# Lo halves of the down weights: a negated copy on ScalarE and an adding DMA in place of VectorE's subtraction

## The chip, the cores and the metric

The kernel runs on one core of one Trainium2 chip. The core has a matrix engine (TensorE, PE in the profile; its weight loads are PEld), VectorE (DVE), ScalarE (ACT), GpSimd (POOL), and SyncE (SP), which issues most of the DMAs. Each engine runs its own instructions in their order and waits on semaphores for the others. 16 DMA engines move data between DRAM and the on-chip memory (SBUF). The metric is the device time of one execution in microseconds, as the median of several runs.

## The reference

A decoder trunk of two layers on 256 tokens of width 1024. Each layer is a SwiGLU FFN, a mixer (causal pooling beside a gated linear recurrence), and a second SwiGLU FFN, each followed by a layer norm. What matters here is the FFN, of which there are four:

```python
D_MODEL = 1024; SEQ = 256; DEPTH = 2
D_FF = ((8 * D_MODEL // 3 + 127) // 128) * 128          # 2816

def swiglu(x, w_gate, w_up, w_down):
    return (jax.nn.silu(x @ w_gate) * (x @ w_up)) @ w_down

# per layer l
x = layer_norm(ALPHA * x + 0.5 * swiglu(x, ffn1_gate[l], ffn1_up[l], ffn1_down[l]), ln_g[l, 0], ln_b[l, 0])
...                                                     # mixer, layer norm
x = layer_norm(ALPHA * x + 0.5 * swiglu(x, ffn2_gate[l], ffn2_up[l], ffn2_down[l]), ln_g[l, 2], ln_b[l, 2])
```

All inputs and the output are float32.

## The kernel before

A float32 operand is split into two float32r halves: hi, the rounded value, and lo, what the rounding left (the value minus hi). A product of two such operands is three matmuls, hi·hi, hi·lo and lo·hi (`mm3`, L95 to L99; the one at L97 reads the lo half of the weight). Everything that PE multiplies, weights above all, is first split in this way by `halves` (L101): ACT writes hi as a rounding copy (L102), DVE writes lo as source minus hi (L103).

Weights come as tiles of 128 x 1024 float32, 512 KB each. Every weight of the program is one `Weight` object, and all of them stand in one list, `stream`, in the order of their use. `advance` (L144) loads from this list as long as the next one finds room, never past one that does not. `Weight.load` (L116) takes a buffer `raw` (five of them, shared by all weights), two buffers for hi and lo from the ring of its kind, issues the load on SP's queue (L128) and splits it (L129). There are three rings: "w" with 8 pairs of buffers (gate and up weights, and the mixer's weights), "x" with 2 more pairs for gate and up weights, and "d" with 6 pairs for the down weights, whose halves are named `dh` and `dl`. A pair comes free when PE has used the weight for both halves of the tokens (`used`, L137).

An FFN (class `FFN`, L289) has 11 groups of 256 hidden columns. Each group needs four gate and up tiles and two down tiles, so there are 22 down tiles in an FFN and 88 in the program. A group's hidden values are made by `GT` (L311, tokens as columns, matmuls at L330) or by `G` (L306, matmuls through `mm3`), pass through `gate_turned` or `gate`, where ACT and DVE compute the silu and the product and split it into `hth` and `htl`, and are multiplied with the down weights in `D` (L452), once for each half of the tokens, into the accumulators `acc`. `D(g, 0)` is the first use of group g's down weights. The first FFN begins with `start` (L375), where pieces of the weights and of x arrive together. In all other FFNs the down weights of groups 0 and 1 are loaded right behind group 1's gate weights; the d ring lies in a scope that is opened anew behind each mixer (`open_ffn`, L149), while the two FFNs that follow one another without a mixer between them share it.

PE's order is written out by hand (`manual_schedule`, L88), with a queue of delayed steps (`Later`, L45) that places transposes and the mixer's small products between the large matmuls. The order on the other engines is planned when the program is built, from priorities and estimated times; loads have a lower priority (`BEHIND`, L145), the gate's instructions a higher one (`AHEAD`, L350). A few splits are pinned to the program's order: the ACT copy for the first ten weights of the stream, and the DVE subtraction of the next few weights after each layer norm (`pinned`, L130 to L134).

GpSimd has little to do: it issues three small DMAs in `lower_bounds` (L563, L565), copies and clears some tiles in the mixer, and computes the power -1/2 in each layer norm (L250) and head norm (L794). The layer norm's last two DVE instructions (L254) wait for that power.

## Time and profile before

| | |
|---|---|
| median of 3 runs | 950.89 us (950.67 to 950.92) |
| span of the profiled execution | 948.8 us |
| what lies around the span, against the median | 2.1 us |
| mean granted clock of TensorE | 0.998 |
| busy: PE, PEld, DVE, ACT, POOL | 99%, 85%, 69%, 54%, 2% of the span |
| DMA | 180.05 MB, mean 190 GB/s; SP's queue 55.6% of 16 engines |

The profile gives no time of the profiled execution beside its span; the difference to the median is taken as what lies around it. "Busy" of an engine is the time in which one of its instructions runs; PE's matmuls overlap, and a matmul of 512 columns takes about 390 ns from start to end while the next starts some 227 ns later. In the rows of a group, the number after the bar is the total busy time in us and the mean duration of one instruction in ns, then the time that its engine was idle before it, and who ended that idleness. In the rows of a timeline the first number is the start in us from the beginning of the span and the second the duration of the row (of all its instructions, where it says x2 or more). In the rows of DMA issues the last number is the median time from issue to landing in us.

### The profile page before, as it was taken

The numbers are of one execution on the slowest core, as the hardware profiler recorded it, in microseconds if no ns is written. First come the engines' busy times: TensorE is split into PE (matmuls) and PEld (weight loads), VectorE is DVE, ScalarE is ACT, GpSimd is POOL, SyncE is SP. The second block draws the span as 40 slices with busy tenths as digits, with TensorE's granted clock in tenths as the row PEclk, the third lists the DMA queues.
The fourth block names the chain that finished last, engine by engine and source line by source line (L and its number), as shares of the span: only waits on it lengthen the run. The fifth ranks groups of instructions, "written<-read, shape, count | busy, mean of one in ns | idle before, by whom it ended". The sixth has DMA issues, their size and how long they took to land.

```text
span 948.8 us, 13285 instructions
## 1 busy us (share of the span) xinstructions
PE 939.1 (99%) x4911; PEld 803.2 (85%) x4911; DVE 653.3 (69%) x1089; ACT 514.7 (54%) x816; POOL 23.7 (2%) x38
## 2 busy tenths in 40 slices
PE   9999999999999999999999999999999999999996
PEld 7888888888988888888888888888898888888885
DVE  7885666669879765655776565647899797565625
ACT  7675554368546755454445645533975466646420
POOL 0000000000010000000000000000000000000000
PEclk9999999999999999999999999999999999999999
DMA  8877676333627876655446666443417387676301
GB/s 309 308 270 261 245 241 195 107 104 118 228 85 257 299 240 208 207 186 178 137 157 237 222 224 208 168 156 101 145 56 264 117 270 253 228 230 211 114 1 45
DMA packets 50944, 180.05 MB, mean 190 GB/s; under 512 B 6208, under 2 KB 6464, under 8 KB 50880
## 3 DMA queue, kind: packets, MB, share of 16 engines
q1 hardware_dynamic: 50544, 178.55, 55.6%
q8 instruction: 38, 0.62, 0.3%
q0 software_dynamic: 192, 0.53, 0.2%
q14 instruction: 26, 0.21, 0.1%
q10 hardware_dynamic: 144, 0.13, 0.0%
HBM read 178.14 MB, written 1.05 MB: 189 GB/s over the span
## 4 chain that ended last, share of the span: by engine, by line
PE 97%; DVE 1%; DMA 1%; ACT 0%; issue 0%; DVEq 0%; ACTq 0%
PE gu L330 39%; PE acc L98 10%; PE acc L97 10%; PE acc L96 10%; PE gu L96 7%; PE gu L97 7%; PE gu L98 7%; PE gu L824 1%; PE acc L405 1%; PE gu L178 1%; PE acc L750 1%; PE acc L696 1%; DMA raw<-in_wout 1%; PE gu L445 0%; PE gu L429 0%; PE acc L786 0%
## 5 line engine op out<-in xcount | busy, mean ns | idle before, releaser
L102 ACT CAST wh<-raw 128x1024 fp32r<-128x1024 f32 x196 | 205.3, 1053 | 114.0 <-DMA raw<-in_gu 45.0
L103 DVE TENSOR_TENSOR wl<-raw,wh 128x1024 fp32r<-128x1024 f32 x196 | 236.1, 1220 | 20.6 <-ACT wh L102 11.7
L330 PE MATMUL gu<-xt,wh 128*128 128x512 f32 x800 | 188.1, 390 | 0.0
L330 PEld LDWEIGHTS gu<-xt,wh 128*128 128x128 f32 x800 | 150.1, 188 | 32.2
L103 DVE TENSOR_TENSOR dl<-raw,dh 128x1024 fp32r<-128x1024 f32 x88 | 106.8, 1223 | 99.2 <-ACT dh L102 98.3
L102 ACT CAST dh<-raw 128x1024 fp32r<-128x1024 f32 x88 | 91.9, 1049 | 113.1 <-DMA raw<-in_dn 109.3
L96 PE MATMUL acc<-dh,hth 128*128 128x512 f32 x354 | 138.8, 392 | 0.0
L98 PE MATMUL acc<-dh,htl 128*128 128x512 f32 x354 | 138.0, 390 | 0.0
L97 PE MATMUL acc<-dl,hth 128*128 128x512 f32 x354 | 137.6, 389 | 0.0
L96 PE MATMUL gu<-wh,xt 128*128 128x512 f32 x288 | 114.2, 396 | 0.0
L97 PE MATMUL gu<-wl,xt 128*128 128x512 f32 x288 | 112.6, 391 | 0.0
L98 PE MATMUL gu<-wh,xt 128*128 128x512 f32 x288 | 112.5, 391 | 0.0
L330 PE MATMUL gu<-xt,wl 128*128 128x256 f32 x800 | 103.5, 282 | 0.0
L330 PEld LDWEIGHTS gu<-xt,wl 128*128 128x128 f32 x800 | 100.6, 191 | 2.1
L353 DVE TENSOR_TENSOR sil<-gu,sil 128x256 f32<-128x256 f32 x66 | 27.8, 421 | 88.4 <-ACT sil L352 88.4
L98 PEld LDWEIGHTS acc<-dh,htl 128*128 128x128 f32 x354 | 66.5, 188 | 13.9
L97 PEld LDWEIGHTS acc<-dl,hth 128*128 128x128 f32 x354 | 66.6, 188 | 12.4
L96 PEld LDWEIGHTS acc<-dh,hth 128*128 128x128 f32 x354 | 66.6, 188 | 12.2
L98 PEld LDWEIGHTS gu<-wh,xt 128*128 128x128 f32 x288 | 54.1, 188 | 11.8 <-DVE xt L103 0.2
L97 PEld LDWEIGHTS gu<-wl,xt 128*128 128x128 f32 x288 | 54.2, 188 | 10.6
L96 PEld LDWEIGHTS gu<-wh,xt 128*128 128x128 f32 x288 | 54.1, 188 | 10.7
L330 PE MATMUL gu<-xt,xh 128*128 128x512 f32 x256 | 62.7, 395 | 0.0
(187 smaller groups left out, 1071.5 us busy)
## 6 DMA issues: line engine op xcount, KB each, us to landing
raw<-in_gu SPq DMA_DIRECT2D x172, 512.0 KB, 4.4
raw<-in_dn SPq DMA_DIRECT2D x88, 512.0 KB, 4.5
raw<-in_win SPq DMA_DIRECT2D x40, 512.0 KB, 4.3
raw<-in_wout SPq DMA_DIRECT2D x16, 512.0 KB, 4.6
lng<-in_ln_g SPq DMA_DIRECT2D x6, 512.0 KB, 4.9
lnb<-in_ln_b SPq DMA_DIRECT2D x6, 512.0 KB, 6.2
x<-in_first SPq DMA_DIRECT2D x4, 384.0 KB, 3.7
raw<-in_first SPq DMA_DIRECT2D x4, 384.0 KB, 4.7
```

The costliest lines, as they stand in the source:

```text
L96: nc.tensor.matmul(ps, lh, wh, start=start, stop=False)
L97: nc.tensor.matmul(ps, lh, wl, start=False, stop=False)
L98: nc.tensor.matmul(ps, ll, wh, start=False, stop=stop)
L102: first = nc.scalar.copy(dst_h, src)
L103: return first, nc.vector.tensor_tensor(dst_l, src, dst_h.bitcast(F32), ALU.subtract)
L178: nc.tensor.transpose(pt[:, k - a, :], self.nat[:, k * P:(k + 1) * P], ident)
L330: nc.tensor.matmul(ps[i][part][:, 2 * S - w:], weight.parts[lo][:, c:c + P], x[:, 0:w], start=kt == 0 and not lo, stop=kt == KT - 1 and lo ...
L353: nc.vector.tensor_tensor(dst, p[:, 0:S], dst, ALU.add)
L405: nc.tensor.matmul(ps[i][part][:, 2 * S - w:], ws[k // 2].parts[lo][:, c:c + P], xs[:, 0:w], start=k == 0 and not lo, stop=k == KT - 1 and ...
L696: nc.tensor.matmul(pe[:, a:], lf[hf][c][:, h * P:(h + 1) * P], cumM[:, c, a:], start=True, stop=True)
L750: nc.tensor.matmul(dst[:, 2 * j:2 * j + 2, :], side[:, j, :], E[:, 2 * j:2 * j + 2, t0:t0 + dst.shape[2]], start=True, stop=True)
L824: nc.tensor.matmul(ps[i // 2][:, i % 2, :], w, x, start=kt == 0 and n == 0 and i % 2 == 0, stop=kt == KT - 1 and n == 2 and i % 2 == 1)
```

## The change

Only the loads of the down weights (ring "d") change. The load of `raw` on SP's queue stays, and ACT's rounding copy into `dh` stays. Then ACT runs a second instruction that reads `dh` and writes it with its sign turned into `dl`, and GpSimd issues a DMA that reads the weight a second time from DRAM and adds it onto `dl` in SBUF. DVE's subtraction is no longer made for these tiles. The gate, up and mixer weights, and the splits of activations, go through `halves` as before. The pinning to the program's order is kept for the ACT copies of the first weights; for the second instruction of a split it now holds only where that is DVE's subtraction.

```diff
             if not self.by_hand:
                 nc.sync.dma_start(raw, self.src)
-                first, second = halves(wh, wl, raw)
-                if position[0] < STARTED + 6:
+                if self.ring == "d":
+                    first = nc.scalar.copy(wh, raw)
+                    if position[0] < STARTED + 6:
+                        tc.keep_in_program_order(first)
+                    nc.scalar.activation(wl, wh.bitcast(F32), AF.Copy, scale=-1.0)
+                    second = nc.gpsimd.dma_start(wl, self.src, accum_op=ALU.add)
+                else:
+                    first, second = halves(wh, wl, raw)
+                if position[0] < STARTED + 6 and isinstance(second.ins, mybir.InstTensorTensor):
                     tc.keep_in_program_order(first)
-                if pinned[0]:
+                if pinned[0] and isinstance(second.ins, mybir.InstTensorTensor):
                     tc.keep_in_program_order(second)
                 pinned[0] = max(0, pinned[0] - 1)
```

## The prediction

> **What bounds the kernel now.** I read the engine totals first, then the chain that ended last, then the waits of TensorE (PE), and only then the places where the changed instructions meet PE. The engine totals and the chain's first line:

> ```profile
> span 948.8 us, 13285 instructions
> PE 939.1 (99%) x4911; PEld 803.2 (85%) x4911; DVE 653.3 (69%) x1089; ACT 514.7 (54%) x816; POOL 23.7 (2%) x38
> ...
> PE 97%; DVE 1%; DMA 1%; ACT 0%; issue 0%; DVEq 0%; ACTq 0%
> ```

> PE is busy for 939.1 of 948.8 us and carries 97% of the chain. The waits view for PE alone has two rows in the whole execution:

> ```profile
> PE gu L429 <- DVE zero L426: 1.1, 1, 1.1
> PE acc L769 <- DVE Pm L762: 0.8, 1, 0.8
> ```

> So PE waited 1.9 us for anybody: 1.1 at the very start, 0.8 in the second mixer. Neither has to do with down weights. Any change that only frees another engine can give back at most those 1.9 us, 0.2% of the time, and a change that makes PE wait anywhere adds that wait in full, because nothing later runs faster to make it up. The question is therefore not how much VectorE (DVE) saves but whether a `dl` now arrives after PE wants it.

> The time is made against the profiled execution: span 948.8, median of the runs 950.89, so 2.1 us lie around the span; I keep them unchanged.

> **What is removed.** The groups by line of the two instructions that make a down weight:

> ```profile
> L103 DVE TENSOR_TENSOR dl<-raw,dh 128x1024 fp32r<-128x1024 f32 x88 | 106.8, 1223 | 99.2 <-ACT dh L102 98.3
> L102 ACT CAST dh<-raw 128x1024 fp32r<-128x1024 f32 x88 | 91.9, 1049 | 113.1 <-DMA raw<-in_dn 109.3
> L354 ACT ACTIVATE sil<-sil 128x256 f32<-128x256 f32 x68 | 28.4, 421 | 5.4 <-DVE sil L353 5.3
> L102 ACT CAST hth<-hn 128x256 fp32r<-128x256 f32 x68 | 27.7, 409 | 18.8 <-DVE hn L355 17.2
> ```

> 88 subtractions of 1223 ns leave DVE: 106.8 us, 653.3 to about 546. PE is never held by them, so their removal is worth 0 on the path. A `raw` buffer of a down weight also comes free at the end of ACT's cast and not of DVE's subtraction, so the SyncE (SP) load queued behind it can start one to three microseconds sooner; PE waits for no load now, so this too is worth 0.

> **What is added.** (a) 88 activations on ScalarE (ACT), 128x1024 each. No row shows that form; the cast of the same size takes 1049 ns, and at 128x256 an ACTIVATE takes 421 against a cast's 409, so I take 1.05, between 1.0 (back to back, where starts overlap) and 1.1. That is 92 us, ACT 515 to 607 of 949. ACT works 9.67 us in the 17 us of a late group (the 416 to 433 stretch below), so two more per group fit there. (b) 88 DMAs on GpSimd (POOL), each behind its activation. (c) 88 times 512 KB more from DRAM, beside the load of `raw`, which stays. The price of (b) is the unknown. The nearest rows, POOL's own DMAs, an SP load of the same 256 KB, the down-weight loads in the first 34 us, and the queue totals:

> ```profile
> 190.66 0.58 POOL L565 DMA_DIRECT2D la<-rows  x1 [2.88 <-DMA rows<-both]
> la<-rows POOLq DMA_DIRECT2D x1, 256.0 KB, 3.6
> pw<-in_pw SPq DMA_DIRECT2D x2, 256.0 KB, 3.9
> raw<-in_dn SPq DMA_DIRECT2D x4, 512.0 KB, 5.0
> q1 hardware_dynamic: 50544, 178.55, 55.6%
> ```

> Call L the time from POOL's issue to the landing of one `dl`. Lower end: 3.6, what a POOL DMA of half the bytes without an add took. Upper end: 10.0, two whole loads of 5.0 one after the other, as if destination and source were fetched in turn. Between them: 55.6% of 948.8 is 527.5 us of all 16 engines for 178.55 MB, so 512 KB (0.524 MB) are 1.55 us of engine time. An addition has to read what it adds to, so I count the crowded load of 5.0 and one more pass of 1.55: L = 6.5. That is nearer the lower end because the two reads should stream together, as the loads do now.

> The two 256 KB rows give POOL's queue no handicap against SP's (3.6 against 3.9). [...]

> **Where it meets PE.** I matched each of the 88 `dl`, in the order of the code, with its first matmul. Three first pairs of the four FFNs come close. The first FFN's (timelines of ACT, DVE, PE):

> ```profile
> 20.54 2.03 ACT L102 CAST dh<-raw 128x1024 fp32r<-128x1024 f32 x2
> 22.74 3.49 DVE L103 TENSOR_TENSOR dl<-raw,dh 128x1024 fp32r<-128x1024 f32 x3
> 27.83 0.40 PE L97 MATMUL acc<-dl,hth 128*128 128x512 f32 x1
> 28.52 0.39 PE L97 MATMUL acc<-dl,hth 128*128 128x512 f32 x1
> ```

> The second `dl` is done near 25.1 now, 3.4 us ahead of 28.52. After the change ACT does two casts and two negations from 20.54, in whichever order: 20.54 + 4 x 1.0 = 24.5. So 4.0 us are left for L: a wait of 6.5 - 4.0 = 2.5 us.

> The FFN behind the first mixer, its first pair, with POOL's row of the layer norm:

> ```profile
> 290.57 1.05 ACT L102 CAST dh<-raw 128x1024 fp32r<-128x1024 f32 x1 [0.44 <-DMA raw<-in_dn]
> 292.26 1.00 POOL L250 TENSOR_TENSOR rs<-rs,neghalf 128x1 f32<-128x1 f32 x1 [13.32 <-DVE rs L249]
> 293.42 1.41 DVE L254 SCALAR_TENSOR_TENSOR x<-x,rs,lnb 128x512 f32<-128x512 f32 x2
> 296.90 1.04 PE L178 MATMUL gu<-ident,x 128*128 128x128 f32 x8
> 292.80 0.39 ACT L363 ACTIVATE sil<-gu 128x256 f32<-128x256 f32 x1
> 298.36 1.22 DVE L103 TENSOR_TENSOR dl<-raw,dh 128x1024 fp32r<-128x1024 f32 x1
> 300.08 0.39 PE L97 MATMUL acc<-dl,hth 128*128 128x512 f32 x1
> ```

> Here DVE finishes the second `dl` at 299.58, only 0.5 us ahead. After the change: 290.57 + 4 x 1.0 + 0.4 for the silu between = 295.0; 5.1 us are left for L, a wait of 1.4 us. The FFN behind the second mixer repeats it:

> ```profile
> 760.10 1.05 ACT L102 CAST dh<-raw 128x1024 fp32r<-128x1024 f32 x1 [0.16 <-DMA raw<-in_dn]
> 769.42 0.39 PE L97 MATMUL acc<-dl,hth 128*128 128x512 f32 x1
> ```

> 760.10 + 4.4 = 764.5, 4.9 left, a wait of 1.6 us. At both places POOL computes a layer norm's power (292.26 to 293.26) just as the first DMA becomes ready (292.6), so that DMA waits 0.65 us; the second pair member sets the wait and is free of it. If the planner puts the DMA first, the power comes about 1.3 us late, and the transposes that need it start at 296.90, 2.1 us after the normalised rows are done now (293.42 + 1.41 = 294.83), so it is covered.

> All other pairs are covered: the next closest are the second pair of the same two FFNs (ready 303.4, used 313.60) and the first pair of the third FFN:

> ```profile
> 301.02 2.36 DVE L103 TENSOR_TENSOR dl<-raw,dh 128x1024 fp32r<-128x1024 f32 x2
> 313.60 0.39 PE L97 MATMUL acc<-dl,hth 128*128 128x512 f32 x1
> 467.42 2.35 DVE L103 TENSOR_TENSOR dl<-raw,dh 128x1024 fp32r<-128x1024 f32 x2
> 484.73 0.39 PE L97 MATMUL acc<-dl,hth 128*128 128x512 f32 x1
> ```

> 10 and 15 us of cover stand against L plus one activation less one subtraction, about 6.4. The loads behind must not starve either. Bandwidth by stretch (columns: stretch, length, busy of PE, PEld, DVE, ACT, POOL, clock, DMA share, GB/s):

> ```profile
> 20.00:40.00 20.00, 20.00 (x105) 17.10 (x104) 18.35 (x23) 14.50 (x23) 0.00 (x0) 1.00 0.82 279
> 416.00:433.00 17.00, 17.00 (x92) 14.69 (x91) 9.93 (x15) 9.67 (x16) 0.00 (x0) 1.00 0.59 199
> ```

> A late group leaves 41% of 17 us, 7.0 us of DMA, for two additions of 1.55 to 3.1 each: it fits. At 20 to 40 us only 3.6 us are free for four additions, so gate weights there land a few microseconds later; PE, itself 2.5 us late, gives them as much back, so I add nothing.

> **Sum.** 2.5 + 1.4 + 1.6 = 5.5 us: span 954.3, time 950.89 + 5.5 = 956.4. With L = 3.6 all three waits vanish, 950.9. With L = 10.0 they are 6.0 + 4.9 + 5.1 = 16.0, 966.9.

> **Rivals.** First, no slower: the added DMA lands as fast as a plain load (L up to 5.0), the second pair member arrives on time behind both mixers, and only the first FFN waits, up to 1.0 us: 950.9 to 951.9. For it: the POOL row of 3.6 and DMA engines that have gaps; against it: that row has half the bytes and no add. It ends where L passes 5.2 (1.2 + 0.1 + 0.3 = 1.6).

> Second, much slower: the adding runs well below the copy rate. An add costing 3.5 us of all engines or more exceeds the 7.0 us free in a late group, `dl` falls behind group by group, and waits like L = 12 (8.0 + 6.9 + 7.1 = 22) give 973 or more. For it: nothing shows the rate of an add; against it: a late `dl` has 10 us of cover and more, so only the three starts and the crowded first FFN would show it.

> [...]

> Fourth, faster: less DVE work removes the 0.8 us wait before L769 and the planner's new order costs nothing: 950.1 at best, since PE cannot do its 939.1 us of work sooner.

> **Chances and range.** The forecast (L 5.2 to 10) 0.55; no slower 0.20; much slower with or without the clock 0.21; faster 0.04, of which hardly any passes the bound. A measurement of this kernel can tell about 0.2%, 1.9 us, from no change. So faster 0.03, same 0.21, slower 0.76. The range runs from just under L = 3.6 to the upper end of L with a first clock loss: 950.7 to 969.

> **What would show it.** Right: PE's waits gain three rows for `dl`, all before the first pair in the FFNs at about 28, 300 and 769 us; DVE near 546, ACT near 607; POOL's issue to landing 5.2 to 10 us; no new PE wait in late groups. Wrong: issue to landing under 5 (then nothing is lost), DMA share near 1.00 in late groups, clock below 1.00 behind a wait, or PE waits for `gu` weights or behind a layer norm, which I priced at nothing.

## The result and the profile after

The changed kernel takes 1023.64 us (median of 4 runs, 1018.12 to 1025.66) against 950.83 us before: a ratio of 1.0755, 95% interval 1.0731 to 1.0780. It is slower, as forecast, but by 72.8 us where 5.5 were forecast, and far above the upper end of the range (969). The profiled execution took 1025.38 us with a span of 1023.6, 74.8 more than the span before.

Engine totals and the DMA queue that grew, from the page after:

```profile
span 1023.6 us, 13365 instructions
...
PE 968.2 (95%) x4911; PEld 816.7 (80%) x4911; DVE 552.0 (54%) x1001; ACT 588.8 (58%) x904; POOL 99.7 (10%) x126
...
q0 software_dynamic: 12864, 46.67, 24.7%
```

PE does the same 4911 matmuls, but is busy for 29.1 us more (968.2 against 939.1) and idle for 45.7 us more (55.4 against 9.7). These two add up to the 74.8. So there are two questions: whom did PE wait for, and why did the same matmuls take longer? Queue q0, GpSimd's, carried 0.53 MB and took 0.2% before. Now 24.7% of 1023.6 us over the 88 adds is 2.87 us of all 16 engines for one add (the few DMAs that were there before make 0.02 us of it).

The two largest rows of PE's waits (before, the view had the two that the prediction shows):

```profile
PE gu L337 <- DVE sil L360: 25.2, 13, 4.6
PE acc L97 <- DMA dl<-in_dn: 20.0, 6, 5.2
...
```

The second row is the one that the prediction has: six waits for `dl`, two in each of the three first pairs, but 20.0 us where 5.5 were forecast. The first row it hasn't: 13 times PE stands before the gate and up matmuls (L337, L330 before the change) because DVE has not yet read the tile `gu` (L360) that they overwrite, in PSUM, the memory that PE writes its results to.

The longer matmuls are a matter of the granted clock. Three stretches behind the three first pairs, PE alone (stretch, length, busy of PE with its count, clock, DMA share, GB/s):

```profile
33.17:43.41 10.24, 7.10 (x16) 0.50 1.05 276
336.95:343.78 6.83, 4.78 (x11) 0.50 1.06 276
831.89:842.13 10.24, 6.70 (x15) 0.50 1.06 276
```

The clock is 0.50 there, and half of the 18.6 us of work, 9.3 us, is lost. Eight more such stretches, 3.41 us each, stand behind gate waits. PE works for 45.2 us in all eleven, so the clock explains 22.6 of the 29.1 us; the other 6.5 are not explained here.

Where the loss accrues is seen when each PE matmul of a `dl` is set against the same one before. Its lateness (us, worked out from the starts of the 354 matmuls L97 in both traces) grows from 0 to 12.1 in the first pairs of the first FFN, to 32.1 at that FFN's end, by 9.1 in the first pairs of the second, 10.4 in the rest of it, 9.3 in the third FFN, 9.2 in the first pairs of the fourth and 5.1 behind them: 75.2 in all. First pairs cost 30.4 of this, the rest 44.8.

How a gate comes late shows in the timelines of ACT and PE in the first FFN:

```profile
93.32 1.05 ACT L130 CAST dh<-raw 128x1024 fp32r<-128x1024 f32 x1 [5.91 <-DMA raw<-in_dn]
94.28 1.04 ACT L102 CAST wh<-raw 128x1024 fp32r<-128x1024 f32 x1
95.22 1.05 ACT L133 ACTIVATE dl<-dh 128x1024 fp32r<-128x1024 f32 x1
...
100.03 0.36 ACT L359 COPY sil<-gu 128x256 f32<-128x256 f32 x1
```

```profile
100.91 1.46 PE L337 MATMUL gu<-xt,wh 128*128 128x512 f32 x3 [3.70 <-DVE sil L360]
```

ACT stands 5.91 us before the cast of a down weight whose load is late. The cast and six more instructions for weights stand in ACT's order ahead of the gate's first copy at 100.03, DVE's part (L360) comes behind that, and PE, which ran out of free `gu` tiles at 97.2, waits 3.70 us. The load that ACT waits for is one of two issued at 84.3 and 84.7 us:

```profile
raw<-in_dn SPq DMA_DIRECT2D x2, 512.0 KB, 10.1
```

Before, the median of these loads was 4.5 us. The DMA engines are full here: their share is 1.00 from 82 to 88 us and 1.05 from 88 to 94 (a packet counts whole in the stretch in which it starts, so a share can pass 1). By stretch of the same work, before and then after (columns as in the prediction's table; the first FFN from its start-up on, and the second, third and fourth FFN):

```profile
20.00:172.00 152.00, 152.00 (x806) 131.05 (x805) 101.80 (x145) 88.07 (x141) 0.00 (x0) 1.00 0.72 245
...
299.00:484.00 185.00, 185.00 (x948) 157.60 (x947) 122.16 (x172) 97.44 (x148) 1.84 (x2) 1.00 0.62 210
484.00:655.00 171.00, 171.00 (x882) 145.91 (x881) 102.50 (x146) 88.24 (x136) 0.92 (x1) 1.00 0.56 188
...
768.00:945.00 177.00, 173.08 (x891) 147.61 (x890) 105.95 (x158) 80.50 (x129) 1.84 (x2) 1.00 0.50 168
```

```profile
20.00:204.00 184.00, 163.13 (x810) 136.66 (x809) 78.07 (x125) 108.88 (x164) 19.52 (x22) 0.94 0.91 268
...
332.00:535.00 203.00, 191.34 (x944) 160.61 (x944) 93.53 (x146) 115.93 (x173) 21.57 (x25) 0.97 0.86 247
535.00:715.00 180.00, 175.09 (x876) 147.38 (x875) 81.45 (x128) 102.80 (x155) 16.64 (x19) 0.98 0.83 240
...
829.00:1020.00 191.00, 178.65 (x887) 150.16 (x887) 81.41 (x136) 95.76 (x149) 18.38 (x21) 0.96 0.75 212
```

Before, the first FFN kept the DMA engines busy for 0.72 x 152 = 109 us. Its 22 adds of 2.87 are 63 more: 172 us of work for 152 us of time. As long as these transfers stay in this stage, some of them land late, whatever order the engines work in.

### The profile page after: what moved, and what is told of

Read it like the earlier page. It is cut to its first block, busy times and chain, and to the rows that moved or that the text cites. A ratio compares the mean times of both kernels' runs of the same rounds, so it can differ in the third digit from the quotient of the medians.

```text
span 1023.6 us, 13365 instructions
## 1 busy us (share of the span) xinstructions
PE 968.2 (95%) x4911; PEld 816.7 (80%) x4911; DVE 552.0 (54%) x1001; ACT 588.8 (58%) x904; POOL 99.7 (10%) x126
## 3 DMA queue, kind: packets, MB, share of 16 engines
q1 hardware_dynamic: 50544, 178.55, 49.7%
q0 software_dynamic: 12864, 46.67, 24.7%
HBM read 224.27 MB, written 1.05 MB: 220 GB/s over the span
## 5 line engine op out<-in xcount | busy, mean ns | idle before, releaser
L102 ACT CAST wh<-raw 128x1024 fp32r<-128x1024 f32 x196 | 205.0, 1048 | 106.6 <-PE gu L98 48.0
L103 DVE TENSOR_TENSOR wl<-raw,wh 128x1024 fp32r<-128x1024 f32 x196 | 236.3, 1221 | 40.1 <-ACT wh L102 30.1
L337 PE MATMUL gu<-xt,wh 128*128 128x512 f32 x800 | 205.0, 412 | 24.5 <-DVE sil L360 23.5
L337 PEld LDWEIGHTS gu<-xt,wh 128*128 128x128 f32 x800 | 158.0, 199 | 66.4 <-DVE sil L360 28.0
L360 DVE TENSOR_TENSOR sil<-gu,sil 128x256 f32<-128x256 f32 x66 | 27.8, 421 | 259.2 <-ACT sil L359 259.2
L97 PE MATMUL acc<-dl,hth 128*128 128x512 f32 x354 | 141.6, 400 | 20.0 <-DMA dl<-in_dn 20.0
L96 PE MATMUL acc<-dh,hth 128*128 128x512 f32 x354 | 141.3, 399 | 0.0
L98 PE MATMUL acc<-dh,htl 128*128 128x512 f32 x354 | 141.0, 398 | 0.0
L134 POOL DMA_DIRECT2D dl<-in_dn x88 | 77.2, 877 | 634.0 <-ACT dl L133 367.7
L97 PE MATMUL gu<-wl,xt 128*128 128x512 f32 x288 | 113.1, 393 | 0.0
L337 PE MATMUL gu<-xt,wl 128*128 128x256 f32 x800 | 103.5, 283 | 0.0
L337 PEld LDWEIGHTS gu<-xt,wl 128*128 128x128 f32 x800 | 100.6, 191 | 2.0
L97 PEld LDWEIGHTS acc<-dl,hth 128*128 128x128 f32 x354 | 68.2, 193 | 35.5 <-DMA dl<-in_dn 22.9
L133 ACT ACTIVATE dl<-dh 128x1024 fp32r<-128x1024 f32 x88 | 92.5, 1056 | 0.7
L337 PE MATMUL gu<-xt,xh 128*128 128x512 f32 x256 | 63.8, 398 | 1.8 <-DVE sil L360 1.8
L98 PEld LDWEIGHTS gu<-wh,xt 128*128 128x128 f32 x288 | 54.4, 189 | 11.8 <-DVE xt L103 0.2
## 6 DMA issues: line engine op xcount, KB each, us to landing
raw<-in_gu SPq DMA_DIRECT2D x172, 512.0 KB, 5.7
raw<-in_dn SPq DMA_DIRECT2D x88, 512.0 KB, 5.1
dl<-in_dn POOLq DMA_DIRECT2D x88, 512.0 KB, 8.6
raw<-in_win SPq DMA_DIRECT2D x40, 512.0 KB, 5.0
raw<-in_wout SPq DMA_DIRECT2D x16, 512.0 KB, 4.6
lng<-in_ln_g SPq DMA_DIRECT2D x6, 512.0 KB, 6.0
lnb<-in_ln_b SPq DMA_DIRECT2D x6, 512.0 KB, 8.2
```

What stands on the lines that cost most here:

```text
L96: nc.tensor.matmul(ps, lh, wh, start=start, stop=False)
L97: nc.tensor.matmul(ps, lh, wl, start=False, stop=False)
L98: nc.tensor.matmul(ps, ll, wh, start=False, stop=stop)
L102: first = nc.scalar.copy(dst_h, src)
L103: return first, nc.vector.tensor_tensor(dst_l, src, dst_h.bitcast(F32), ALU.subtract)
L133: nc.scalar.activation(wl, wh.bitcast(F32), AF.Copy, scale=-1.0)
```

## The experiments

Two theories and a rival stood at the start. L: the first adds of an FFN land too late (the `dl` row). T: the traffic of the adds makes later loads late, and through ACT's order the gate. O: the 88 extra ACT instructions and the planner's new order make the gate late without any traffic. Each experiment is told with its change to the changed kernel, unless it says otherwise. All were timed beside the kernel before on the same chip.

**No DMA, the negation kept.**

```diff
-                    second = nc.gpsimd.dma_start(wl, self.src, accum_op=ALU.add)
+                    second = nc.vector.tensor_tensor(wl, raw, wl.bitcast(F32), ALU.add)
```

> The changed kernel, but VectorE adds the loaded weight onto the negated tile; no added DMA. ACT keeps its second instruction for each down weight, and the planner orders ACT and DVE anew. Theory T (traffic: the adding DMAs make later loads of raw late, ACT stands in order before a cast that waits for its load, the gate behind it is late, TensorE waits for a free PSUM bank) and theory L (the first adds of an FFN land too late): neither has anything left here, so 951 to 955. Rival O (ACT's 88 extra instructions and the new order on ACT and DVE make the gate late by themselves): the waits of PE for the gate stay, 26 us of them and some 13 us of half clock behind them, so 980 to 992.

The two conditions on pinning ask for `self.ring != "d"` in this kernel, so that the same instructions are pinned as in the changed kernel. 952.28 us, ratio 1.0016 (1.0006 to 1.0025). The page and the waits:

```profile
PE 940.1 (99%) x4911; PEld 802.6 (84%) x4911; DVE 653.0 (69%) x1089; ACT 589.2 (62%) x904; POOL 23.7 (2%) x38
```

```profile
PE gu L337 <- DVE sil L360: 0.2, 1, 0.2
```

ACT has the work that it has in the changed kernel (589.2 against 588.8), and the gate waits are 0.2 us. The extra ACT instructions cost 1.5 us at most. The planner's order is another one here, since DVE has its 88 instructions back, so the half of O that blames the order is left to the copy below.

**An eighth of each add.**

```diff
-                    second = nc.gpsimd.dma_start(wl, self.src, accum_op=ALU.add)
+                    second = nc.gpsimd.dma_start(wl[:, 0:128], self.src[:, 0:128], accum_op=ALU.add)
```

> The changed kernel, but each adding DMA covers columns 0 to 127 of 1024, so that the output leaves out seven eighths of the addition: the same instructions on the same engines, an eighth of the bytes. T: the DMA share falls back near that of before and the waits for the gate go; L: an add lands in 3 to 5 us, the waits for dl go; both together 951 to 957. O: the waits for the gate stay, 980 to 992. If the dl waits come from the way GpSimd issues (a fixed cost per DMA) and not from bytes, issue to landing stays above 8 us and about 34 us of the loss stay: 985.

960.46 us, ratio 1.0097 (1.0082 to 1.0112): above the 957 of T and L, far below the 980 of O. The waits for the gate are gone, those for `dl` not wholly; O's 88 ACT instructions are all still there (waits of PE, then DMA issues):

```profile
PE acc L97 <- DMA dl<-in_dn: 5.0, 6, 2.5
```

```profile
raw<-in_gu SPq DMA_DIRECT2D x172, 512.0 KB, 4.7
raw<-in_dn SPq DMA_DIRECT2D x88, 512.0 KB, 4.3
dl<-in_dn POOLq DMA_DIRECT2D x88, 64.0 KB, 4.2
```

A DMA of 64 KB still takes 4.2 us, nearly as long as the loads of 512 KB. So the latency behind the first waits is only partly one of its own bytes.

**A copy instead of an add.**

```diff
-                    second = nc.gpsimd.dma_start(wl, self.src, accum_op=ALU.add)
+                    second = nc.gpsimd.dma_start(wl, self.src)
```

> The changed kernel, but the DMA copies the weight over the negated tile instead of adding, so that the subtraction is left out: the same reads from DRAM, the same order, no read of the destination. If the price is the addition itself (2.87 us of all 16 engines against 1.5 for a copy): DMA share near 0.80 in late groups, issue to landing 5 to 6 us, most waits go: 952 to 965. If the price is the second read from DRAM, of whatever kind: little changes, 1005 to 1025. In between: the waits at the three starts go by half (L about 6 to 8) and the gate waits stay, 985.

975.30 us, ratio 1.0255 (1.0236 to 1.0275), between the low case and the middle one. Of the middle case the first half came (the waits for `dl` fall from 20.0 to 11.8 us), the second did not (the gate waits nearly go) (the page's queue and DMA issue, then the waits of PE):

```profile
q0 software_dynamic: 12864, 46.67, 14.8%
...
dl<-in_dn POOLq DMA_DIRECT2D x88, 512.0 KB, 6.5
```

```profile
PE acc L97 <- DMA dl<-in_dn: 11.8, 6, 3.3
PE gu L337 <- DVE sil L360: 3.1, 2, 2.5
```

14.8% of 972.3 us over 88 is 1.64 us of engine time for a copy, against 2.87 for an add of the same bytes. That the DMA adds, and does not only copy, is worth 1023.6 - 975.3 = 48.3 of the 72.8 us. ACT, DVE and GpSimd run the same instructions in the same order in this kernel as in the changed one (904, 1001 and 126, compared place by place in the two traces). So neither the order nor ACT's negations, both of which are still there, can account for the 48.3 us, and O falls.

The landing of the second member ends the waits of a first pair. Its issue to landing in the first, second and fourth FFN, first with the add, then the copy, then the eighth of an add (each one DMA):

```profile
dl<-in_dn POOLq DMA_DIRECT2D x1, 512.0 KB, 10.7
...
dl<-in_dn POOLq DMA_DIRECT2D x1, 512.0 KB, 11.1
...
dl<-in_dn POOLq DMA_DIRECT2D x1, 512.0 KB, 12.4
```

```profile
dl<-in_dn POOLq DMA_DIRECT2D x1, 512.0 KB, 7.7
...
dl<-in_dn POOLq DMA_DIRECT2D x1, 512.0 KB, 8.3
...
dl<-in_dn POOLq DMA_DIRECT2D x1, 512.0 KB, 9.3
```

```profile
dl<-in_dn POOLq DMA_DIRECT2D x1, 64.0 KB, 5.9
...
dl<-in_dn POOLq DMA_DIRECT2D x1, 64.0 KB, 6.0
...
dl<-in_dn POOLq DMA_DIRECT2D x1, 64.0 KB, 6.3
```

Means of 11.4, 8.4 and 6.1: of 11.4 us some 6 are there with an eighth of the bytes, 2.3 more come with the rest of the bytes and 3.0 with adding instead of copying. Why 64 KB take 5.9 to 6.3 us at these places was not isolated.

**The first two groups of each FFN without the add.**

```diff
-                if self.ring == "d":
+                if self.ring == "d" and not self.soon:
...
-                    self.dw[n] = [Weight(dn[2 * n + i], "d", ND) for i in range(2)]
+                    self.dw[n] = [Weight(dn[2 * n + i], "d", ND, soon=n < 2) for i in range(2)]
```

> The changed kernel, but the first four down weights of each FFN get their lo half from VectorE as before (16 of 88); the other 72 keep the adding DMA. L and T are separate losses: the 20.0 us of waits for dl and the 13.7 us of half clock behind them go, the waits for the gate stay: about 990. If the waits for dl cause the others too (everything later is displaced by them): 955 to 970. If removing them gains nothing, because the loads behind were only hidden by these waits: 1010 or more.

995.50 us, ratio 1.0465 (1.0436 to 1.0493), within 6 us of the first case:

```profile
PE gu L338 <- DVE sil L361: 28.5, 14, 5.4
```

No wait for `dl` is left, and the gate waits (one line further down in this kernel) are about as they were, 28.5 us against 25.2. L and T are separate: 28 us for the first pairs, by lateness 30.4, and 44.7 for the rest, by lateness 44.8.

**The traffic alone.** The kernel before, and beside it an add (then a copy) of each down weight onto a spare tile:

```diff
                 first, second = halves(wh, wl, raw)
+                if self.ring == "d":
...
+                    extra = nc.gpsimd.dma_start(spare, self.src, accum_op=ALU.add)
+                    tc.add_manual_dep(extra.ins, first.ins.name,
...
```

> The kernel before, whole, and besides it for each down weight an adding DMA from GpSimd's queue, issued behind ACT's rounding copy, onto a spare tile that nobody reads; one spare tile, so an add starts when the one before it has landed. ACT has no second instruction, and nothing waits for the adds. If the traffic of the adds alone makes the loads, and through ACT's order the gate, late: waits of PE for the gate of 15 to 30 us and half clock behind them, 970 to 995. If the loads become late but VectorE's old share of the work and the old order absorb it (the loss needs ACT's negation standing between cast and gate as well): 951 to 958.

> As the run with the spare add, with a plain copy in place of the add: the same bytes from DRAM, about half the engine time. If it is the time that the DMA engines spend, and not the bytes from DRAM, that makes the loads late: 951 to 955, whatever the spare add shows. If the bytes: as the spare add within 5 us.

1050.48 us (ratio 1.1059, 1.1005 to 1.1114) and 986.74 us (1.0382, 1.0329 to 1.0435): the traffic alone costs more than the change. The waits of PE with the add, then with the copy:

```profile
PE gu L341 <- DVE sil L364: 46.6, 28, 4.6
PE gu L456 <- DVE hn L375: 15.1, 3, 13.3
```

```profile
PE gu L341 <- DVE sil L364: 11.6, 10, 2.6
PE gu L456 <- DVE hn L375: 9.2, 3, 6.9
```

With ACT's and DVE's old work and nobody waiting for the adds, the gate waits come in full: the traffic alone makes the gate late, as T has it. Both numbers missed, though: the add is above the range, and the copy is not 951 to 955, so engine time alone does not decide. Part of the excess belongs to the experiment: with one spare tile each DMA waits on POOL for the one before, and a layer norm's power stands behind it. In the run with the add:

```profile
548.84 0.88 POOL L133 DMA_DIRECT2D spare<-in_dn  x1 [5.11 <-DMA spare<-in_dn]
549.40 0.90 POOL L261 TENSOR_TENSOR rs<-rs,neghalf 128x1 f32<-128x1 f32 x1
```

That is the 13.3 us in the row for `hn`. The larger gate waits (46.6 against 25.2) fit with `raw`, which here comes free only after DVE's subtraction, while the changed kernel frees it behind ACT's cast; that was not isolated.

**Half of the adds.** The kernel without adds in the first two groups, and of every other pair only the second weight keeps its add.

```diff
-                    self.dw[n] = [Weight(dn[2 * n + i], "d", ND, soon=n < 2) for i in range(2)]
+                    self.dw[n] = [Weight(dn[2 * n + i], "d", ND, soon=n < 2 or i == 0) for i in range(2)]
```

> The kernel in which the first four down weights of each FFN go through VectorE (995.5), and of the others only the second of each pair keeps the adding DMA: 36 adds, not 72. If each add costs its share (44.7 us for 72): 973. If the loss begins where the DMA engines are full (share 0.9 and more in the late groups, which 36 adds bring to about 0.75): 951 to 960.

962.75 us, ratio 1.0120 (1.0090 to 1.0151): 12.0 us for 36 adds where 72 cost 44.7. It lies 2.8 us above the full-engine case and 10 below the case of equal shares.

Four kernels can now be set against the filling of the DMA engines. For each FFN, need is the DMA time before plus its adds or copies by their engine time (2.87; 1.64 for a copy; 3.07 in the last kernel, from 11.5% of 962.0 us over 36), over the FFN's time before; the loss is the growth of the lateness without the first pairs:

| kernel | first FFN | second | third | fourth |
|---|---|---|---|---|
| changed | 1.13: 20.0 us | 0.96: 10.4 | 0.93: 9.3 | 0.86: 5.1 |
| no adds in the first two groups | 1.06: 18.6 | 0.90: 9.0 | 0.86: 11.6 | 0.79: 7.0 |
| copy | 0.96: 3.9 | 0.81: 0.0 | 0.77: 0.2 | 0.70: 0.0 |
| every other add | 0.90: 8.6 | 0.77: 0.1 | 0.72: 3.9 | 0.66: 1.2 |

Above 1 the loss is heavy. Between 0.7 and 1 the mean does not decide alone: in these four kernels adds lose where copies at the same filling do not; why was not tested by itself. The spare copies, which are not in the table, do not fit it: at the copy's filling of 0.96 they lost 12.2 us in the first FFN, 7.7 of it in waits for the gate, where the copy lost 3.9. So the filling is not all that counts; what else does was not isolated.

**The waits filled with work.** In the first, second and fourth FFN, ahead of the first pair:

```diff
+                    if g == 0 and hf == 0 and c == 0 and self.ln != (1, 0):
+                        for _ in range((14, 9)[i]):
+                            nc.tensor.matmul(self.accs[hf][1], ht[i][0], dw[i][0][:, cs], start=True, stop=True)
                     mm3(self.accs[hf][c], ht[i][0], ht[i][1], dw[i][0][:, cs], dw[i][1][:, cs],
```

> The changed kernel, with more work for PE: in the first, second and fourth FFN 14 more matmuls ahead of the first pair of down weights and 9 ahead of its second member (3.2 and 2.0 us at 0.227 us each), into an accumulator that is cleared before its use; the output stays the same. They fit into waits for dl of 5.2 and 2.2, 3.2 and 2.8, 4.4 and 2.2 us. If the granted clock is halved because PE stood idle: the spells of 10.2, 6.8 and 10.2 us at half clock behind these waits go, which is worth half of 27.3: 1010 to 1013 from 1023.6, less work per time but sooner. If the half clock comes from something else that goes on there (the DMA burst, the load on the chip): 1023 to 1026, spells as before. If the fillers only add: 1030 or more.

1025.98 us, ratio 1.0774 (1.0724 to 1.0823). The time is that of "something else", the trace is not:

```profile
PE 976.8 (95%) x4980; PEld 823.7 (80%) x4980; DVE 551.3 (54%) x1001; ACT 589.9 (57%) x904; POOL 100.3 (10%) x126
```

```profile
PE gu L337 <- DVE sil L360: 34.7, 15, 7.7
PE acc L97 <- DMA dl<-in_dn: 5.0, 5, 2.2
```

Behind the first pairs 3.4 us at half clock are left of 27.3. PE is busy for 8.6 us more with 69 more matmuls of 0.227 us (15.7 us), so 7.1 us of clock came back, of 9.3 by PE's work (the expectation took half of all 27.3 us); but the gate waits grew by 9.5 us, most of them in the first FFN (7.7 us at 76.7). With the loads setting the pace there, the earlier PE only waited for longer.

**The same, with the copy.** There the first FFN's filling is 0.96, not 1.13.

```diff
+                        for _ in range((9, 7)[i]):
+                            nc.tensor.matmul(self.accs[hf][1], ht[i][0], dw[i][0][:, cs], start=True, stop=True)
```

> The kernel with a copy in place of the add (975.3; it leaves out the subtraction), with 9 and 7 more matmuls of PE ahead of the first pair of down weights in the first, second and fourth FFN (2.0 and 1.6 us), into an accumulator that is cleared before its use. There the waits for dl were 3.3 and 1.0, 1.6 and 1.6, 2.8 and 1.6 us and half clock behind them cost about half of 13.5 us of work. Now the DMA engines have room in the first FFN, unlike in the changed kernel with filled waits. If standing idle halves the clock: spells shrink from 17.1 us to 6.8 or less, PE busy without the fillers falls by 4 to 7 us, and little of it is given back: time 970 to 974, though 48 matmuls (10.9 us) are added. If idleness is not the cause: spells as before and 976 to 980, since the fillers do not fit wholly. If every lead gained is given back at the gate: 975 to 980 with spells gone.

967.18 us, ratio 1.0184 (1.0161 to 1.0206), against 975.30 with 48 matmuls fewer: more work, and 8 us sooner, below even the range.

```profile
PE 951.3 (99%) x4959; PEld 811.4 (84%) x4959; DVE 551.3 (57%) x1001; ACT 589.4 (61%) x904; POOL 70.6 (7%) x126
```

Without the 10.9 us of fillers PE is busy for 940.4 us, 7.8 less than in the copy kernel and 1.3 more than before, and no stretch at half clock is left before the end: the mean granted clock is 0.998, as before the change, against 0.99 in the copy kernel. With PE's idleness filled, the half clock went.

**A longer descriptor space.** In the changed kernel the fourth add of an FFN is issued only when the first lands (in the first FFN ready at 31.8 us, issued at 34.3, the first landed at 34.1).

```diff
-    nc = bacc.Bacc("TRN2", target_bir_lowering=False, num_devices=1, dynamic_dma_scratch_size=1024)
+    nc = bacc.Bacc("TRN2", target_bir_lowering=False, num_devices=1, dynamic_dma_scratch_size=4096)
```

> The changed kernel with four times the space for the descriptors of GpSimd's DMAs (4096 in place of 1024), so that a fourth add need not wait for the landing of the first. If the DMA engines' time sets the loss: 1019 to 1030, with the fourth add of an FFN issued earlier but landing no earlier. If GpSimd's queue held adds back: 990 to 1010.

1025.48 us, ratio 1.0795 (1.0751 to 1.0840), no change:

```profile
PE gu L337 <- DVE sil L360: 24.3, 13, 4.6
PE acc L97 <- DMA dl<-in_dn: 17.8, 6, 4.8
```

The fourth add is now issued at once (31.6) and takes 13.0 us instead of 11.2; in both kernels it lands 11.4 to 11.5 us behind the first. GpSimd's queue did hold its issue back, but that cost nothing: issued 2.7 us sooner, the add landed no sooner behind the first.

## Why the prediction was right and wrong, point by point

- **PE's waits as the question, and the three places: right.** All waits for `dl` are in the three first pairs, and the third FFN has none.
- **L: mis-sized.** The term that failed is L = 6.5, and its upper bound of 10.0 too: 10.7 to 12.4 were measured. 6.5 is the median of a copy, and even copies took 7.7 to 9.3 at the first pairs. Two things were missed: at the first pairs the DMA engines were full (share 1.03 from 27.2 to 37.9 us, from 328 to 339 and from 824.5 to 837; even 64 KB took 5.9 to 6.3 us there), and the row that I took for the lower end came from a time when the DMA engines were less than half busy (0.44 from 190.5 to 194.5 us).
- **The margins: right at two places, too wide at the first.** With the L that was measured, the prediction's own formula gives 10.7 - 4.0, 11.1 - 5.1 and 12.4 - 4.9, that is 6.7, 6.0 and 7.5: 20.2 us. 7.4, 6.0 and 6.6 came, 20.0. That the sums agree so well is partly luck. The prediction had ACT done with the first pair at 24.5, "in whichever order", but ACT took the cast of a third weight ahead of the second negation:

```profile
23.96 1.98 ACT L130 CAST dh<-raw 128x1024 fp32r<-128x1024 f32 x2
25.85 1.05 ACT L133 ACTIVATE dl<-dh 128x1024 fp32r<-128x1024 f32 x1
...
27.21 0.88 POOL L134 DMA_DIRECT2D dl<-in_dn  x1 [1.79 <-ACT sil L359]
```

So the second DMA was issued at 27.21 (about 1 us of that was lost ahead of any down weight: the cast that begins at 13.82 before begins at 14.91 after). Against that, PE's matmuls between the two waits of a pair ran at half clock (0.50 from 33.17 to 43.41 us), so that part of the delay does not show as a wait.

- **The add's engine time, "1.55 to 3.1": 2.87, near the upper end.** The bound held; what was done with it did not.
- **"A late group ... it fits" and, for the first FFN, "gate weights there land a few microseconds later ... I add nothing": the step that failed most.** I weighed one late group (0.59) and the 20 us of the start, but never the whole first FFN: with my own upper price 22 x 3.1 + 109 = 177 us of DMA in 152 would have stood there. At the start PE's own lateness covered for the loads, as I wrote (its first wait for the gate ends at 80.6 us), but the lack goes on for the whole FFN. This crowding cost 44.8 us, with its share of half clock.
- **What is behind a late load.** I looked for PE waiting for weights. PE waited for the gate, since ACT runs in order: a cast that waits for its load holds the gate's copies. The prediction named PE's `gu` waits as a sign that would prove it wrong; that sign came, through another engine.
- **DVE's saving worth nothing: right as far as the runs tell** (552.0 us busy; PE's waits before left only 1.9 us to win, and no run takes the saving alone). **ACT's 88 instructions fit: right**, 1.5 us by the run without the DMA.
- **The clock, which the sum leaves out: wrong.** PE's busy time grew by 29.1 us, of which 22.6 are the clock's, 9.3 of them behind the first pairs. The range's upper end, 969, holds "a first clock loss", 2.1 us above the 966.9 of L = 10.0; no run shows that term. What the runs showed in its place is a clock of 0.50 for 10.24, 6.83 and 10.24 us behind the three first pairs, and for 3.41 us at each of the eight other places, where PE had idled for 1.51 to 2.91 us in the 3.41 us before.
- **The rival "much slower" came closest.** It named an add well below the copy rate and L = 12. The add took 2.87 against 1.64, though not the 3.5 that the rival asked for, and L was 10.7 to 12.4. Its price of 22 us for the first pairs is near the 20.0 measured. Its `dl` that falls behind group by group did not come: PE waited for none behind the first pairs; its "973 or more" had no term for the gate and none for the clock, which made the rest.

What stays open: how much of the 44.8 us would go if ACT took the gate ahead of the casts. That was not tried.

## What to carry to other kernels

Before a DMA is put in place of an engine's instruction, sum the DMA engines' time over every stage whole, at the upper price of the new transfer, and compare it with the stage's length; a mean over the run or one roomy stretch hides the stage that overflows. Nor was a sum just below the stage's length safe here: the fourth FFN, at 0.86, still lost 5.1 us. A late load costs more than its own consumer: it holds whatever stands behind its cast in an in-order engine (here ACT stood 5.91 us before a cast, and PE 3.70 us for the gate behind it). And where TensorE sits idle, look at the granted clock behind it: in the changed kernel it fell to 0.50 for 3.41 us or more at eleven places, on top of the waits. Filling the waits with matmuls gained 8 us in the copy kernel (967.18 against 975.30) and nothing in the changed one (1025.98 against 1023.64), where loads set the pace.

## What the runs showed of the hardware that I had not expected

```profile
L134 POOL DMA_DIRECT2D dl<-in_dn x88 | 77.2, 877 | 634.0 <-ACT dl L133 367.7
```

```profile
L134 POOL DMA_DIRECT2D dl<-in_dn x88 | 47.8, 544 | 611.4 <-ACT dl L133 407.5
```
